# Sliding-window attention: whole weights against the preceding values, a difference of values for the block's own, sinks as a 129th column, queries spread by transfers

## Chip, core and metric

One core of a Trainium2 chip runs the whole two-layer network in one launch. The metric is the device time of the launch in microseconds (us), median of several runs; everything is float32 or its rounded matmul form float32r ("fp32r").

## What is computed

The program is a two-layer decoder over 1024 tokens of width 1024: a gated linear recurrence with a gated convolutional FFN, then sliding-window attention with a second such FFN. The change touches only the attention of layer 2:

```
q = (h @ w_q)                          # 16 heads of 64; keys and values are shared by 4 heads each
for each block of 128 queries:         # keys of this block and of the block before it
    logits = q k^T / 8 + bias[dist]    # only keys at distance 0..127 count
    m      = max(logits.max(), sink)   # one learned sink per head
    p      = exp(logits - m)
    o      = (p @ v) / (p.sum() + exp(sink - m))
out = o @ w_out
```

A query at place t of its block sees keys 0..t of its own block and keys t+1..127 of the block before: exactly 128 keys in all. So one 128x128 tile per block and head holds all the weights, and each column s of it belongs to the own block where s <= t and to the preceding block where s > t.

## The kernel before

**Precision.** A float32 product is three fp32r matmuls (`mm3`) of a rounded high part and a low part of each operand; a low part is made by VectorE (DVE) as source minus high part (L149), the high part by a cast on ScalarE (ACT). Products of weights and values are plain float32 matmuls (`mm32`, L180).

**Attention, by head pairs and block pairs.** `c` (0 to 7) counts pairs of heads, `e` is the head in the pair (partitions 64e to 64e+63), `bp` (0 to 3) counts pairs of 128-query blocks. A step is n = 4c + bp, 32 in all. `attend(c, bp, q)` is a generator of seven stages for a step:

1. TensorE (PE): scores of 2 heads x 2 blocks in a PSUM tile (L1212, 8 matmuls; operands `q` and `QB` are the stationary ones); ACT copies the own block's half to the tile `X` (L1215).
2. DVE lays the preceding block's scores over it where s > t (`copy_predicated`, L1219); GpSimd (POOL) adds the bias (L1225). For bp = 0 there is a block with no predecessor, cut by an `affine_select`.
3. DVE: row maxima (L1230), and a small operation that takes the sink in (L1233); POOL, or DVE for c > 5, forms sink minus maximum (L1234); ACT: four exponentials with row sums in `dn` (L1237), one of the sinks (L1239).
4. DVE adds the sink's part to `dn` (L1241), takes the reciprocal and multiplies `X` (L1243).
5. PE transposes `X` four times into a PSUM tile `pt` (L184).
6. DVE multiplies `pt` by two triangles (L1251, twice): weights of the own block in `W[:, 0]`, of the preceding one in `W[:, 1]`.
7. PE multiplies both by the values `Vt` (16 matmuls, L180); ACT copies the result to `Y` (L1264).

**Order.** PE, ACT, DVE and POOL run in the order written in the code. In step n stand: stage 1 of n, stage 7 of n-3, stage 3 of n-1, stage 2 of n, stages 5 and 6 of n-2, half of a filler, stage 4 of n-1, `q_split` if a query half is done, `make_lows` (deferred low parts), at bp = 0 `q_unit(c+2)`, the other half of the filler. Filler is the projection of the queries of c+1: six matmuls of 512 columns at a time; half h of it ends two steps after it began. After step 20 there is more of the next stage's work: weights of the output projection (`out_unit`, steps 21 to 24) and splits of `Y` (`Y_to_T`, steps 26 to 30). SyncE (SP) issues the DMAs; its order is the scheduler's.

**Queries.** `q_split` takes a projected half from PSUM (head e in partitions 64e..) and makes two stationary operands: `q[:, e]` holds the high part of head e in both partition halves, `QB[:, e]` the low part in one half and zeros in the other. `K` has the high part of the keys in head e's partitions and the low part in the others, so two matmuls give the three products. That is two ACT copies, two DVE operations and two ACT copies more, each on 64 partitions (L1195, L1197, L1200). Half 0 of c+1 is split in step 4c+2 and first used in step 4c+4; half 1 is split in step 4c+4 and used in step 4c+6.

**Weights.** `q_unit` loads the weights of one c by SP into one of three tiles `raw` in turn (`load`, L144), ACT casts them to a slot of `HL` (L156), and DVE makes the low part in the next step's `make_lows`. `HL` has six slots, handed out by `ring["hl"]`.

Of the kernel before, what the change touches and what calls it, by code (L numbers as in the profile page):

```python
# [35 lines left out]
def constant_arrays():  # L36
# [9 lines left out]
    tri = np.zeros((P, 2, P), np.float32)  # L46
    tri[:, 0] = s <= t
    tri[:, 1] = s > t
# [39 lines left out]
def trunk(ctx: ExitStack, tc: tile.TileContext, a: dict, out: bass.AP):  # L88
# [21 lines left out]
    cp.tile([P, 88], F32, name="pad1")  # L110
# [29 lines left out]
    def load(loads):  # L140
        raw = tail["raw"][ring["raw"] % 3]
        ring["raw"] += 1
        for view, src in loads(raw):
            nc.sync.dma_start(view, src)  # L144
        return raw
# [956 lines left out]
    with (tc.tile_pool(name="ta", bufs=1, reuse_waits="tile") as raws,  # L1102
# [7 lines left out]
        tri = at.tile([P, 2, P], F32, name="tri")  # L1110
# [3 lines left out]
        nsk = at.tile([P, 16], F32, name="nsk")  # L1114
        nc.gpsimd.tensor_scalar(nsk, sk, -1.0, None, op0=ALU.mult)
        at.tile([P, 96], F32, name="pad")
        place["hf"] = lambda tb: at.tile([P, KC, P], F32, name="q", bufs=3)
        rows = []
        for v in (a["ln_ffn_g"][0], a["ln_ffn_b"][0]):
            rows.append([at.tile([P, 512], F32, name="X", bufs=4) for _ in range(2)])  # L1120
# [5 lines left out]
        Vt = at.tile([P, NB, 256], F32, name="Vt")  # L1126
        khl, uv = [], []
# [63 lines left out]
        def q_split(q, ps):  # L1191
            heads = [(slice(64 * e, 64 * e + 64), slice(64 - 64 * e, 128 - 64 * e)) for e in range(2)]
            qh, ql = q
            for e, (es, os) in enumerate(heads):
                nc.scalar.activation(qh[es, e, :], ps[es], AF.Copy, scale=0.125)  # L1195
            for e, (es, os) in enumerate(heads):
                nc.vector.scalar_tensor_tensor(ql[es, e, :], ps[es], 0.125, qh[es, e, :].bitcast(F32),  # L1197
                                               op0=ALU.mult, op1=ALU.subtract)
            for e, (es, os) in enumerate(heads):
                nc.scalar.activation(qh[os, e, :], ps[es], AF.Copy, scale=0.125)  # L1200

        def attend(c, bp, q):
# [11 lines left out]
            X = at.tile([P, 2, 2, P], F32, name="X", bufs=4)  # L1214
            nc.scalar.copy(X, pv[:, :, :, P:])  # L1215
            yield
# [11 lines left out]
            se = sm.tile([P, 2, 2], F32, name="se")  # L1228
            dn = sm.tile([P, 2, 2], F32, name="dn")
            nc.vector.tensor_reduce(nm, X, axis=mybir.AxisListType.X, op=ALU.max)  # L1230
            skv = sk[:, 8 * pp + r:8 * pp + r + 5:4].unsqueeze(2).to_broadcast([P, 2, 2])
            nsv = nsk[:, 8 * pp + r:8 * pp + r + 5:4].unsqueeze(2).to_broadcast([P, 2, 2])
            nc.vector.scalar_tensor_tensor(nm, nm, -1.0, nsv, op0=ALU.mult, op1=ALU.min)  # L1233
            (nc.vector if c > 5 else nc.gpsimd).tensor_tensor(se, skv, nm, op=ALU.add)  # L1234
            for e in range(2):
                for jj in range(2):
                    nc.scalar.activation(X[:, e, jj, :], X[:, e, jj, :], AF.Exp, bias=nm[:, e, jj:jj + 1],  # L1237
                                         accum_out=dn[:, e, jj:jj + 1])
            nc.scalar.activation(se, se, AF.Exp)  # L1239
            yield  # L1240
            nc.vector.tensor_tensor(dn, dn, se, op=ALU.add)  # L1241
# [8 lines left out]
            for k in range(2):  # L1250
                nc.vector.tensor_tensor(W[:, k], pt.rearrange("p (g s) -> p g s", g=4),  # L1251
# [46 lines left out]
        def make_lows():  # L1298
            while lows:
                lows.pop(0)()  # L1300
# [119 lines left out]
```

## Time and profile before

| | us |
|---|---|
| median of 3 runs (2201.86 to 2205.51) | 2202.15 |
| the profiled execution, its own time | 2201.14 |
| its span, first to last instruction | 2199.3 |
| attention's steps: first scores at 1284.06, last scores at 1462.80 | 178.7 |

PE is busy for 98% of the span, DVE 81%, ACT 43%, POOL 8%; PE's granted clock is 0.999 of full speed. PE's busy time is a union of overlapping matmuls: a 512-column matmul is shown as 0.39 us long while the next begins 0.23 us later, so a short wait between two can lie under the end of the first. Times below are from the span's start.

### The profile page before, as it was taken

To read this page: it belongs to the slowest core of one execution; us is meant where nothing else is said; L and a number is where in the kernel's file an instruction comes from. 1 tells how busy PE (TensorE), PEld (TensorE's weight loads), DVE (VectorE), ACT (ScalarE), POOL (GpSimd) and SP (SyncE) were. 2 spreads that over 40 slices of the span, in tenths; PEclk is the share of its full clock that TensorE was granted. 3 is DMA by queue.
4 is the path that set the end of the run, shared out by engine and by line. 5 is a ranking of instruction groups with operands and counts; after the bars stand their busy time and mean duration, and the time that the engine had idled before them with its cause. 6 is when DMAs were issued, how large, how long until landed. Compare 5 with 4: busy or idle time off the path is not lost.

```text
span 2199.3 us, 33413 instructions
## 1 busy us (share of the span) xinstructions
PE 2154.9 (98%) x13135; PEld 1813.7 (82%) x13135; DVE 1782.7 (81%) x2415; ACT 942.3 (43%) x1625; POOL 179.3 (8%) x200
## 2 busy tenths in 40 slices
PE   8999999999999999999999999999999999999998
PEld 7888888978888888887888888778788888887887
DVE  2777666565789988888998778887799888889987
ACT  4333322342744433344344356764654443343431
POOL 0122111120100000000000012211000000000001
PEclk9999999999999999999999999999999999999999
DMA  5554443152222222238854421114222222249663
GB/s 198 191 194 173 154 173 116 59 127 93 86 82 86 87 86 86 87 99 271 281 168 134 115 90 35 35 56 140 74 96 94 77 78 87 87 147 318 205 215 134
DMA packets 231945, 281.16 MB, mean 128 GB/s; under 512 B 29978, under 2 KB 160747, under 8 KB 228971
## 3 DMA queue, kind: packets, MB, share of 16 engines
q1 hardware_dynamic: 228736, 276.53, 38.3%
q10 hardware_dynamic: 3050, 2.49, 0.9%
q8 instruction: 103, 1.69, 0.3%
q14 instruction: 56, 0.45, 0.1%
HBM read 213.96 MB, written 65.01 MB: 127 GB/s over the span
## 4 chain that ended last, share of the span: by engine, by line
PE 68%; DVE 18%; ACT 5%; DMA 4%; issue 3%; POOL 1%; SPq 0%; ACTq 0%; DVEq 0%; POOLq 0%
PE psmm L174 14%; PE psmm L176 14%; PE psmm L175 14%; PE psax L174 7%; PE psax L176 7%; PE psax L175 7%; PE psax L180 3%; DVE T L149 3%; DVE HL L149 2%; DVE Y L647 1%; PE psax L184 1%; ACT T L201 1%; DMA rx<-in_ffn_w_in_dram 1%; ACT Y L249 1%; DVE Y L599 1%
## 5 line engine op out<-in xcount | busy, mean ns | idle before, releaser
L174 PE MATMUL psmm<-T,HL 128*128 128x512 f32 x768 | 306.9, 400 | 0.0
L175 PE MATMUL psmm<-T,HL 128*128 128x512 f32 x768 | 299.4, 390 | 4.2 <-DVE T L149 2.8
L176 PE MATMUL psmm<-T,HL 128*128 128x512 f32 x768 | 299.5, 390 | 0.0
L479 DVE SCALAR_TENSOR_TENSOR Y<-Y,cwt 128x1023 f32<-128x1023 f32 (+1 forms) x176 | 225.1, 1279 | 39.5 <-ACT Y L477 39.3
L477 ACT ACTIVATE Y<-Y,cwt 128x1024 f32<-128x1024 f32 x88 | 108.9, 1238 | 257.4 <-DVE Y L466 254.5
L174 PE MATMUL psmm<-HL,T 128*128 128x256 f32 (+1 forms) x656 | 199.7, 304 | 2.4 <-ACT T L201 2.4
L176 PE MATMUL psmm<-HL,T 128*128 128x256 f32 (+1 forms) x656 | 195.2, 298 | 2.4 <-DVE T L149 2.4
L175 PE MATMUL psmm<-HL,T 128*128 128x256 f32 (+1 forms) x656 | 195.0, 297 | 1.2 <-DVE HL L149 1.2
L201 ACT CAST HL<-rx 128x1024 fp32r<-128x1024 f32 (+1 forms) x137 | 140.3, 1047 | 122.0 <-DMA rx<-in_ffn_w_in_dram 33.6
L149 DVE TENSOR_TENSOR HL<-rx,HL 128x1024 fp32r<-128x1024 f32 (+1 forms) x137 | 165.6, 1212 | 15.3 <-ACT HL L201 14.9
L176 PEld LDWEIGHTS psmm<-T,HL 128*128 128x128 f32 x768 | 144.2, 188 | 32.5 <-issue 1.7
L175 PEld LDWEIGHTS psmm<-T,HL 128*128 128x128 f32 x768 | 144.5, 188 | 30.9 <-DVE T L149 3.5
L174 PEld LDWEIGHTS psmm<-T,HL 128*128 128x128 f32 x768 | 144.3, 188 | 30.3 <-issue 1.2
L174 PE MATMUL psax<-T,HL 128*128 128x512 f32 x352 | 137.3, 390 | 0.0
L176 PE MATMUL psax<-T,HL 128*128 128x512 f32 x352 | 137.0, 389 | 0.0
L175 PE MATMUL psax<-T,HL 128*128 128x512 f32 x352 | 136.9, 389 | 0.0
L174 PEld LDWEIGHTS psmm<-HL,T 128*128 128x128 f32 x656 | 126.1, 192 | 9.2 <-ACT T L201 3.0
L176 PEld LDWEIGHTS psmm<-HL,T 128*128 128x128 f32 x656 | 126.0, 192 | 6.6 <-DVE T L149 3.4
L175 PEld LDWEIGHTS psmm<-HL,T 128*128 128x128 f32 x656 | 126.2, 192 | 4.9 <-DVE HL L149 1.7
L223 POOL TENSOR_TENSOR rs<-rs,nhalf 128x1 f32<-128x1 f32 x32 | 25.7, 805 | 1281.1 <-DVE rs L222 1280.8
L858 POOL TENSOR_TENSOR kp<-kp,tot 128x512 f32<-128x512 f32 x48 | 73.8, 1538 | 288.3 <-PE psax L180 147.9
L201 ACT CAST HT<-rx 128x1024 fp32r<-128x1024 f32 (+1 forms) x51 | 44.0, 862 | 89.0 <-PE psmm L175 29.9
(296 smaller groups left out, 5312.7 us busy)
## 6 DMA issues: line engine op xcount, KB each, us to landing
rx<-in_ffn_w_in_dram SPq DMA_DIRECT2D x136, 256.0 KB, 3.2
rx<-gd SPq DMA_DIRECT2D x118, 256.0 KB, 3.6
Y<-in_ffn_w_out_dram SPq DMA_DIRECT2D x44, 512.0 KB, 6.4
bsd<-Y SPq DMA_DIRECT2D x22, 1024.0 KB, 4.4
gd<-Y SPq DMA_DIRECT2D x44, 512.0 KB, 2.6
rx<-in_ffn_w_out_dram SPq DMA_DIRECT2D x54, 256.0 KB, 4.1
R<-bsd SPq DMA_DIRECT2D x44, 256.0 KB, 4.4
Y<-in_ffn_w_in_dram SPq DMA_DIRECT2D x40, 256.0 KB, 3.0
```

Source lines behind the costliest of these rows:

```text
L149: make = lambda e: e.tensor_tensor(lo, src, hi.bitcast(F32), op=ALU.subtract)
L174: nc.tensor.matmul(ps, st(0), mv(0), start=start, stop=False)
L175: nc.tensor.matmul(ps, st(0), mv(1), start=False, stop=False)
L176: nc.tensor.matmul(ps, st(1), mv(0), start=False, stop=stop)
L180: nc.tensor.matmul(ps, lhsT, rhs, start=start, stop=stop, **kw)
L184: nc.tensor.transpose(ps, src, ident)
L201: nc.scalar.copy(hi, src)
L223: nc.gpsimd.tensor_tensor(rs, rs, nhalf, op=ALU.pow)
L249: nc.scalar.activation(hf[:, kc, :], ps[:, k * P:(k + 1) * P], AF.Identity, bias=shift, scale=scale)
L477: nc.scalar.activation(c, u, AF.Identity, bias=cwt[:, l, 3, ci:ci + 1], scale=cwt[:, l, 2, ci:ci + 1])
L479: nc.vector.scalar_tensor_tensor(c[:, sh:], u[:, :S - sh], cwt[:, l, 2 - sh, ci:ci + 1], c[:, sh:], op0=ALU.mult, op1=ALU.add)
L858: (nc.gpsimd if i else nc.vector).tensor_tensor(kv[:, :, 0, :], kv[:, :, 0, :], tv[:, :, 1:2].to_broadcast([P, nb, m]), op=ALU.mult)
```

## The change

Weights: with p the whole tile, the output is p @ V_prev + (own part of p) @ (V_own - V_prev). So `W[:, 1]` becomes a plain copy of `pt` by ACT, `W[:, 0]` stays DVE's product with a triangle, and the own block's values are replaced by a difference `Vd`, which POOL makes once. PE's first matmul of a pair now takes `W[:, 1]`, and the number of matmuls is the same.

Sinks: `X` gets a 129th column, written by POOL, which holds the sink; the maximum runs over 129 columns and is negated by the operation itself, and the exponential's row sum takes the sink in. L1233, L1234, L1239 and L1241 go.

Queries: ACT copies the high part of both heads to a tile `M` at once, DVE makes the low part of both in `L` at once, and six SP transfers of 64 partitions x 512 carry them to their places in `q` and `QB`. `M` and `L` are the halves of one of the three `raw` tiles, so two are left for the weights; `QB` moves to slot 5 of `HL`, so five slots are left and the slots are handed out in another sequence.

```
-        raw = tail["raw"][ring["raw"] % 3]
+        raw = tail["raw"][ring["raw"] % len(tail["raw"])]
...
-        QB = [at.tile([P, 2, 512], F32R, name=f"QB{i}") for i in range(2)]
-        for t in QB:
-            for e in range(2):
-                nc.gpsimd.memset(t[64 - 64 * e:128 - 64 * e, e, :].bitcast(F32), 0.0)
+        QB = [hl_at(5)[:, i, :].rearrange("p (e t) -> p e t", e=2) for i in range(2)]
...
+        Vd = at.tile([P, NB - 1, 256], F32, name="Vd")
...
+            j0 = max(2 * tp, 1)
+            nc.gpsimd.tensor_tensor(Vd[:, j0 - 1:2 * tp + 1, :], Vt[:, j0:2 * tp + 2, :], Vt[:, j0 - 1:2 * tp + 1, :],
+                                    op=ALU.subtract)
...
-            ring["hl"] = (2, 3, 4, 5, 0, 1, 4, 5)[c]
+            ring["hl"] = (2, 3, 4, 0, 1, 2, 3, 4)[c]
...
         def q_split(q, ps):
-            heads = [(slice(64 * e, 64 * e + 64), slice(64 - 64 * e, 128 - 64 * e)) for e in range(2)]
             qh, ql = q
-            for e, (es, os) in enumerate(heads):
-                nc.scalar.activation(qh[es, e, :], ps[es], AF.Copy, scale=0.125)
-            for e, (es, os) in enumerate(heads):
-                nc.vector.scalar_tensor_tensor(ql[es, e, :], ps[es], 0.125, qh[es, e, :].bitcast(F32),
-                                               op0=ALU.mult, op1=ALU.subtract)
-            for e, (es, os) in enumerate(heads):
-                nc.scalar.activation(qh[os, e, :], ps[es], AF.Copy, scale=0.125)
+            M, L = [place["ML"][:, 512 * i:512 * i + 512] for i in range(2)]
+            nc.scalar.activation(M.bitcast(F32R), ps, AF.Copy, scale=0.125)
+            nc.vector.scalar_tensor_tensor(L.bitcast(F32R), ps, 0.125, M, op0=ALU.mult, op1=ALU.subtract)
+            for e in range(2):
+                es, os = slice(64 * e, 64 * e + 64), slice(64 - 64 * e, 128 - 64 * e)
+                for dst, src in ((qh[es, e, :], M), (qh[os, e, :], M), (ql[es, e, :], L)):
+                    nc.sync.dma_start(dst.bitcast(F32), src[es])
...
-            X = at.tile([P, 2, 2, P], F32, name="X", bufs=4)
+            XS = at.tile([P, 2, 2, 144], F32, name="X", bufs=4)
+            X, XS = XS[:, :, :, :P], XS[:, :, :, :P + 1]
             nc.scalar.copy(X, pv[:, :, :, P:])
+            nc.gpsimd.tensor_copy(XS[:, :, :, P], sk[:, 8 * pp + r:8 * pp + r + 5:4].unsqueeze(2).to_broadcast([P, 2, 2]))
...
-            nc.vector.tensor_reduce(nm, X, axis=mybir.AxisListType.X, op=ALU.max)
...
-            nc.vector.scalar_tensor_tensor(nm, nm, -1.0, nsv, op0=ALU.mult, op1=ALU.min)
-            (nc.vector if c > 5 else nc.gpsimd).tensor_tensor(se, skv, nm, op=ALU.add)
+            nc.vector.tensor_reduce(nm, XS, axis=mybir.AxisListType.X, op=ALU.max, negate=True)
...
-                    nc.scalar.activation(X[:, e, jj, :], X[:, e, jj, :], AF.Exp, bias=nm[:, e, jj:jj + 1],
+                    nc.scalar.activation(XS[:, e, jj, :], XS[:, e, jj, :], AF.Exp, bias=nm[:, e, jj:jj + 1],
                                          accum_out=dn[:, e, jj:jj + 1])
-            nc.scalar.activation(se, se, AF.Exp)
             yield
-            nc.vector.tensor_tensor(dn, dn, se, op=ALU.add)
...
-            for k in range(2):
-                nc.vector.tensor_tensor(W[:, k], pt.rearrange("p (g s) -> p g s", g=4),
-                                        tri[:, k, :].unsqueeze(1).to_broadcast([P, 4, P]), op=ALU.mult)
+            nc.vector.tensor_tensor(W[:, 0], pt.rearrange("p (g s) -> p g s", g=4),
+                                    tri.unsqueeze(1).to_broadcast([P, 4, P]), op=ALU.mult)
+            nc.scalar.copy(W[:, 1], pt.rearrange("p (g s) -> p g s", g=4))
...
-                    mm32(o, Vt[:, j, kvc:kvc + 64], W[:, 0, 2 * e + jj, :], stop=j == 0)
+                    mm32(o, Vt[:, max(j - 1, 0), kvc:kvc + 64], W[:, 1, 2 * e + jj, :], stop=j == 0)
                     if j:
-                        mm32(o, Vt[:, j - 1, kvc:kvc + 64], W[:, 1, 2 * e + jj, :], start=False)
+                        mm32(o, Vd[:, j - 1, kvc:kvc + 64], W[:, 0, 2 * e + jj, :], start=False)
...
             hl = q_unit(1)
             make_lows()
+            place["ML"] = tail["raw"][ring["raw"] % 3]
+            tail["raw"] = [t for t in tail["raw"] if t is not place["ML"]]
```

How the instructions stand now is shown at three places. The first is ACT's queue in step 8, a step with a query split. Before:

```order
L1215 COPY X<-psax 128x512
L1264 COPY Y<-psmm 128x256
L1237 ACTIVATE X,dn<-X,nm 128x128 x4
L1239 ACTIVATE se<-se 128x4
L1195 ACTIVATE q<-psmm 64x512 x2
L1200 ACTIVATE q<-psmm 64x512 x2
L156 CAST HL<-raw_10081 128x1024
```

In the changed kernel the same step on ACT, with the engines or DMA semaphores that each instruction waits for in brackets (`raw_10082` is the tile of `M` and `L`):

```order
L1212 COPY X<-psax 128x4x128 [waits PE_49]
L1255 COPY Y<-psmm 128x256 [waits PE_49]
L1230 ACTIVATE X,dn<-X,nm 128x129 [waits DVE_49]
L1230 ACTIVATE X,dn<-X,nm 128x129 x3
L1243 COPY Y<-psmm 128x512 [waits DVE_49,Activation_49]
L1191 ACTIVATE raw_10082<-psmm 128x512 [waits DMAHW6_49,DMAHW4_49,DMAHW7_49,DMAHW3_49,Activation_49]
L154 CAST HL<-raw_10081 128x1024 [waits DMAHW2_49]
```

The exponential of the sinks and four query copies went; a copy of the transposed weights, which waits for DVE's product from the same PSUM tile, and one query copy, which waits for the four transfers that read `M` last, came. The second place is DVE's queue in such a step. Before:

```order
L1230 TENSOR_REDUCE nm<-X 128x4
L1233 SCALAR_TENSOR_TENSOR nm<-nm,nsk 128x4
L1219 COPY_PREDICATED X<-msk,psax 128x128 x2
L1251 TENSOR_TENSOR Y<-psmm,tri 128x512 x2
L1241 TENSOR_TENSOR dn<-dn,se 128x4
L1242 RECIPROCAL dn<-dn 128x4
L1243 TENSOR_TENSOR X<-X,dn 128x512
L1197 SCALAR_TENSOR_TENSOR QB_10086<-psmm,q 64x512 x2
```

and in the changed kernel:

```order
L1227 TENSOR_REDUCE nm<-X 128x4
L1217 COPY_PREDICATED X<-msk,psax 128x128 x2
L1241 TENSOR_TENSOR Y<-psmm,tri 128x512
L1233 RECIPROCAL dn<-dn 128x4
L1234 TENSOR_TENSOR X<-X,dn 128x4x128
L1192 SCALAR_TENSOR_TENSOR raw_10082<-psmm,raw_10082 128x512
```

Two small operations went, the product with a triangle and the query operation stand once in place of twice, and the order is otherwise the same. The third place is SP's queue around one step in four: loads of the bias (`bf`) and of the query weights. Before:

```order
L272 DMA h2d<-Y 128x1024 x3
L144 DMA raw_10082<-in_swa_w_q_dram 128x8x64 x2
L1162 DMA bf<-rbd 128x2x128
L144 DMA raw_10083<-in_swa_w_q_dram 128x8x64 x2
L1162 DMA bf<-rbd 128x2x128
L144 DMA raw_10081<-in_swa_w_q_dram 128x8x64 x2
```

and in the changed kernel (`HL<-raw_10082` is `QB`, now a slot of `HL`):

```order
L1159 DMA bf<-rbd 128x2x128
L1196 DMA q<-raw_10082 64x512 x2
L1196 DMA HL<-raw_10082 64x512
L1196 DMA q<-raw_10082 64x512 x2
L1196 DMA HL<-raw_10082 64x512
L142 DMA raw_10083<-in_swa_w_q_dram 128x8x64 x2
```

The six transfers of a split stand in the program's order between the loads, and the loads use two tiles in turn in place of three.

More of the change, by code (lines that the diff above doesn't have):

```diff
@@ L1119, in trunk @@
         for v in (a["ln_ffn_g"][0], a["ln_ffn_b"][0]):
-            rows.append([at.tile([P, 512], F32, name="X", bufs=4) for _ in range(2)])
+            rows.append([at.tile([P, 576], F32, name="X", bufs=4)[:, :512] for _ in range(2)])
             for h in range(2):
@@ L1315, in trunk @@
             k_part(1)
+            for e in range(2):
+                nc.gpsimd.memset(hl_at(5).rearrange("p i (e t) -> p i e t", e=2)[64 - 64 * e:128 - 64 * e, :, e, :]
+                                 .bitcast(F32), 0.0)
             g = q_proj(hl)
```

15 lines of the change are left out of this document (4 added, 11 removed).

## Prediction

> **What bounds the kernel now.** I read the page first, then the windows of the attention, the waits there, and the starts of the score matmuls in PE's timeline. The windows give, for each stretch: its length, then busy time of PE, its weight loads, DVE, ACT and POOL, PE's granted clock, the DMA share and GB/s.
>
> ```profile
> 1307.00:1331.00 24.00, 23.51 (x177) 19.54 (x176) 20.21 (x45) 16.43 (x57) 7.03 (x11) 1.00 0.12 29
> 1427.00:1451.00 24.00, 21.41 (x151) 17.56 (x151) 22.24 (x46) 17.43 (x54) 6.06 (x6) 1.00 0.00 1
> 1463.00:1475.00 12.00, 11.43 (x88) 8.98 (x87) 10.48 (x23) 7.13 (x24) 1.29 (x1) 1.00 0.00 0
> 1283.00:1475.00 192.00, 183.82 (x1298) 153.43 (x1297) 163.91 (x349) 132.53 (x430) 51.51 (x72) 1.00 0.11 32
> ```
>
> PE is nearly full, at full clock; its visible gaps are 192.00 - 183.82 = 8.2 us. DVE is the engine nearest to it, and in steps 24 to 29 (second row) it works 22.24 of 24 us, with PE down to 21.41. The waits say who holds whom (total us, times, longest):
>
> ```profile
> ACT q L1200 <- DVE QB L1197: 23.2, 15, 1.7
> ACT X L1237 <- DVE nm L1233: 20.3, 15, 2.4
> DVE X L1219 <- ACT X L1215: 16.4, 13, 1.9
> PEld psmm L180 <- DVE W L1251: 7.5, 15, 1.3
> PE psmm L180 <- DVE W L1251: 4.0, 10, 1.1
> ```
>
> PE waits for one thing above all: the weights `W` from DVE. Ahead of it lies a chain: ACT waits inside the query split for DVE, comes late to the copy of X, DVE waits for that copy and makes W late. All PE lost is seen in the starts of the scores:
>
> ```profile
> 1306.49 0.22 PE L1212 MATMUL psax<-K,q 128*128 128x128 f32 x1
> 1311.84 0.28 PE L1212 MATMUL psax<-K,q 128*128 128x256 f32 x1
> 1323.29 0.28 PE L1212 MATMUL psax<-K,q 128*128 128x256 f32 x1
> 1328.45 0.22 PE L1212 MATMUL psax<-K,q 128*128 128x128 f32 x1
> 1357.24 0.28 PE L1212 MATMUL psax<-K,q 128*128 128x256 f32 x1
> 1358.28 1.14 PE L180 MATMUL psmm<-Y,Vt 128*64 128x128 f32 x16
> 1359.36 0.66 PE L184 MATMUL psmm<-ident,X 128*128 128x128 f32 x4
> 1362.61 0.28 PE L1212 MATMUL psax<-K,q 128*128 128x256 f32 x1
> 1396.22 0.22 PE L1212 MATMUL psax<-K,q 128*128 128x128 f32 x1
> 1462.80 0.28 PE L1212 MATMUL psax<-K,q 128*128 128x256 f32 x1
> ```
>
> These are steps 4, 5, 7, 8, 13 (three rows), 14, 20 and 31. Without a wait a step takes 1311.84 - 1306.49 = 5.35 us from bp 0, 1362.61 - 1357.24 = 5.37 from bp 1 and bp 2, and 1328.45 - 1323.29 = 5.16 from bp 3, so four take 21.25. From step 4 to step 31 that makes 6 x 21.25 + 5.35 + 2 x 5.37 = 143.6 us; the trace has 1462.80 - 1306.49 = 156.3. **12.7 us are waits**, 4.7 of them before step 20 (89.7 against 85.0) and 8.0 after. They are more than the visible gaps, since a short wait hides under the modelled end of a matmul. PE's own work does not shrink, so 12.7 us, and some 1.5 us of gaps behind step 31, are all that can be won.
>
> **What goes and what comes, engine by engine.** The rows of the groups (count | busy us, mean ns):
>
> ```profile
> L1197 DVE SCALAR_TENSOR_TENSOR QB<-psmm,q 64x512 fp32r<-64x512 f32 x30 | 20.6, 685 | 1.7 <-ACT q L1195 1.2
> L1251 DVE TENSOR_TENSOR Y<-psmm,tri 128x512 f32<-128x512 f32 x32 | 20.5, 683 | 0.0
> L1241 DVE TENSOR_TENSOR dn<-dn,se 128x4 f32<-128x4 f32 x32 | 9.6, 301 | 3.1 <-ACT se L1239 2.9
> L1233 DVE SCALAR_TENSOR_TENSOR nm<-nm,nsk 128x4 f32<-128x4 f32 x32 | 5.2, 163 | 1.1
> L1200 ACT ACTIVATE q<-psmm 64x512 fp32r<-64x512 f32 x30 | 17.8, 594 | 23.6 <-DVE QB L1197 23.2
> L1195 ACT ACTIVATE q<-psmm 64x512 fp32r<-64x512 f32 x30 | 17.6, 586 | 1.7 <-PE psmm L176 1.6
> L1239 ACT ACTIVATE se<-se 128x4 f32<-128x4 f32 x32 | 6.2, 193 | 0.0
> L1215 ACT COPY X<-psax 128x512 f32<-128x512 f32 x32 | 18.7, 585 | 3.7 <-PE psax L1212 3.4
> L1237 ACT ACTIVATE X<-X,nm 128x128 f32<-128x128 f32 x128 | 49.9, 395 | 20.4 <-DVE nm L1233 20.3
> ```
>
> DVE loses half of L1197 (10.3 us), one product of the two (20.5), L1241 (9.6) and L1233 (5.2): 45.6 of 163.9 us, and in a step with a split 0.69 + 0.68 + 0.30 + 0.16 = 1.8 us. ACT loses L1200, half of L1195 and L1239 (17.8 + 8.8 + 6.2 = 32.8) and gains 32 copies of 128x512, priced by L1215 (18.7): 14.1 us less. What matters more is that ACT no longer waits for DVE inside the split (23.2 us), so the cast and the next copy of X come some 3 us earlier in a step with a split. The 129th column adds 1 part in 128 to L1237 and the maximum, under 0.01 us each. POOL's sink copy stands for L1234; four differences of values and two memsets fall into stretches in which POOL is at 7.03 of 24. If that cover went, each costs about what POOL's bias addition of like size does, and four of those are no more than 5 us once.
>
> Does PE then run without waits? I walk one step, T being the start of its scores. PE by the rows of step 13: values at T+1.04, transposes T+2.12 to 2.78, next scores T+5.37. ACT: copy of X T+1.15 to 1.74, copy of Y behind the values T+2.2, four exponentials at 0.39 each T+2.5 to 4.1, copy of the weights T+4.1 to 4.7, M (starts are 0.5 apart) T+4.6 to 5.2. DVE: product with the triangle T+2.8 to 3.5, reciprocal behind the exponentials, X multiplied by T+5.1, L T+5.2 to 5.9. The next step's PE wants the weights at T+5.37+1.04 = 6.4 (ready 4.7) and the transposes' X at 7.5 (ready 5.1). So 1.7 and 2.4 us of slack take the place of the wait for W. The copy of the weights waits for DVE's product from the same PSUM tile, done at 3.5, before ACT is free at 4.1: nothing.
>
> **The transfers are what is late next.** Behind M on SP stand six issues of 64x512, 128 KB each, and no row shows one from SBUF to SBUF. The nearest are the loads of `swa_w_out`, of the same 64x512 shape; the other rows are ends (issue: ns min/median/max; the DMA rows: KB, us from issue to landing):
>
> ```profile
> L144 SPq DMA_DIRECT2D raw<-in_swa_w_out_dram x16: 465/588/596, 1366.3 to 1419.7; - x16
> L272 SPq DMA_DIRECT2D h2d<-Y x8: 319/320/339, 1240.3 to 1291.0; - x8
> 1366.30 2.46 SPq L144 DMA_DIRECT2D raw<-in_swa_w_out_dram  x4
> raw<-in_swa_w_out_dram SPq DMA_DIRECT2D x16, 128.0 KB, 2.6
> rx<-in_swa_w_out_dram SPq DMA_DIRECT2D x16, 128.0 KB, 3.8
> out_dram<-Y SPq DMA_DIRECT2D x2, 256.0 KB, 2.0
> ```
>
> Four issues in 2.46 us, the last 0.59 long, are 0.62 apart. So the first starts at T+5.2, the sixth at T+8.3, and it lands at T+10.9. It is needed two steps on, by the third score matmul (0.26 in, eight take 1.04): at T+10.98 from bp 0 (5.35 + 5.37) and T+10.79 from bp 2 (5.37 + 5.16). That is just in time, 0.1 late in half of the 14 splits inside the loop: +0.7 us. By the ends of the rows the sixth lands between T+9.5 (issues of 0.32 behind L, landing 2.6) and T+12.1 (0.62 and 3.8); I take the row of the same shape.
>
> The Trainium skill (DMA: Bandwidth & Descriptors, Anatomy of one DMA) gives about 2.0 us fixed plus the bytes over 436 GB/s, for another issuing engine; for 128 KB that is an estimate of 2.3 us. By it no split would be late and the sum would be 0.7 us lower; the row's 2.6 decides.
>
> Two places cost more, once each. **The start:** nothing but the other half's projection covers the first split.
>
> ```profile
> 1278.82 1.20 ACT L1195 ACTIVATE q<-psmm 64x512 fp32r<-64x512 f32 x2 [3.19 <-PE psmm L176]
> 1280.05 1.41 DVE L1197 SCALAR_TENSOR_TENSOR QB<-psmm,q 64x512 fp32r<-64x512 f32 x2 [0.16 <-ACT q L1195]
> ```
>
> L ends at 1280.74, the third issue follows, the sixth starts at 1282.6 and lands at 1285.2, against first scores at 1284.06 + 0.26: +0.9. **Two raw tiles for three, steps 22 to 24:** the third load of output weights waits for its tile until DVE's low part late in step 22, stands on SP behind that step's split (until T+8.9, T of step 22), issues for 2.46 us and lands at about T+13.4. ACT wants to cast it at T+10.1 and stands 3.3 us, the next split's M is some 2 us late, and so are the scores of step 26: +2.0.
>
> **The sum.** -12.7 + 0.7 + 0.9 + 2.0 = -9.1 us. Behind the attention PE's work and the loads, which start at its end, only move with it. From the profiled execution's own time 2201.14 that gives 2192.0. That execution lies 1.0 us under the median of the runs, 2202.15, so for a median I say **2193.0**.
>
> **The rivals.**
> A, slower: the queries land late. With 3.8 us to land, the loads' price when other transfers are in flight, the sixth lands at T+12.1, 1.2 us late on the mean in 14 splits (17), the start costs 2.1 and the two tiles 3.2: -12.7 + 17 + 2.1 + 3.2 = +9.6, 2211.7. It decides from a landing of about 3.15 us on, where each split is 0.55 late. For it: no row shows such a transfer, and the slack is nil. Against: DMA share is 0.12, and all sixteen loads in the attention took about 2.6. Chance 0.20.
> B, cheap transfers: issues of 0.32 apart. All 14 splits land in time, the start costs 0.1 and the two tiles 1.2: -11.4, 2190.7. Chance 0.20.
> C, the gain stays under other waits (the order of ACT and DVE on one PSUM tile, POOL's bias, a PSUM slot): if half of 12.7 remains, -6.4 + 3.6 = -2.8, 2199.3. Against: the slacks above. Chance 0.12.
> D, the six transfers go one after the other, each landing before the next moves: 6 x 2.6 behind T+5.2 is T+20.8, 9.9 late, 14 times: about 2340. Against: the four issues of 2.46 us with 2.6 to land each. The Trainium skill (DMA: Bandwidth & Descriptors, Rules for kernel authors) says that transfers to two partition halves serialize on the shared engines; the four loads go to two halves and show no such time. Chance 0.02.
>
> **How the numbers follow.** The forecast has 0.46. A measurement here can tell about 0.2%, 4.4 us, from no change. Faster: forecast and B, 0.66; same: C, 0.12; slower: A and D, 0.22. The range runs from 2188 (all 12.7 and the 1.5 behind step 31 won) to 2210 (C, and A up to near its price); about half of A and all of D, 0.12, lie above it.
>
> **What would show it.** Right: steps of 5.2 to 5.4 us, DVE under 19 of 24, no wait of L180 for W, the split's sixth transfer landing within 0.3 us of the scores, one long step at 25. Wrong: scores waiting a microsecond or more for DMA in every second step (A); scores never near the landing (B); transposes or values waiting for ACT's copy, or steps still near 5.65 (C).

## The result, and the profile after

The changed kernel takes 2198.11 us (median of 11 runs, 2196.49 to 2202.84) against 2203.38 for the kernel before in the same sessions (11 runs, 2201.86 to 2206.31). The ratio is 0.9976, with a 95% interval of 0.9967 to 0.9985: 5.3 us faster, between 3.3 and 7.3. Forecast were 9.1 us, in the same direction.

The profiled execution of the changed kernel has 2199.59 us and a span of 2197.8, only 1.5 us under that of the kernel before. At its last scores it was 5.3 us ahead (1457.52 against 1462.80). It lost most of its lead in the second feed-forward part, where the kernels do the same work: by the count of matmuls still to come it was 5.8 us ahead at 1980 us and 1.5 at 2010. In the windows of the changed kernel there (length, busy PE, weight loads, DVE, ACT, POOL, granted clock, DMA share, GB/s) one stretch stands out:

```profile
1980.00:1990.00 10.00, 10.00 (x46) 8.29 (x45) 9.96 (x10) 3.16 (x3) 0.00 (x0) 1.00 0.98 361
1990.00:2000.00 10.00, 7.42 (x25) 5.44 (x24) 8.22 (x8) 3.14 (x3) 0.00 (x0) 0.77 0.82 278
```

PE runs 25 matmuls in place of 46 and the clock is granted at 0.77. The 11 runs of this one kernel spread over 6.4 us. So I compare kernels by the ratios of their medians, and look inside the attention by the distance of one score matmul to the next, which such a place later on does not touch.

The attention's windows:

```profile
1307.00:1331.00 24.00, 22.88 (x165) 19.24 (x164) 15.54 (x30) 14.33 (x49) 7.32 (x12) 1.00 0.50 116
...
1427.00:1451.00 24.00, 22.76 (x160) 18.77 (x159) 18.70 (x35) 17.46 (x58) 8.39 (x11) 1.00 0.37 87
...
1283.00:1475.00 192.00, 185.60 (x1330) 156.16 (x1329) 127.00 (x233) 120.82 (x386) 56.05 (x81) 1.00 0.43 107
```

DVE falls from 163.91 to 127.00 us, ACT from 132.53 to 120.82, and PE is busy for 1.8 us more of the same 192. DVE in the late stretch stands at 18.70 of 24, where it was 22.24. The waits of the same part (total us, times, longest):

```profile
PEld psmm L178 <- ACT Y L1243: 2.6, 2, 1.8
PE psax L1208 <- DMA q<-raw: 2.3, 5, 0.9
PE psmm L178 <- ACT Y L1243: 2.2, 2, 1.6
PE psax L1208 <- DMA HL<-raw: 1.4, 5, 0.4
```

No wait of the values (L178, before L180) for DVE is left. In its place stand waits for ACT's copy of the weights and ten for transfers. The score starts in PE's timeline:

```profile
1283.33 0.22 PE L1208 MATMUL psax<-K,q 128*128 128x128 f32 x1
...
1307.67 0.22 PE L1208 MATMUL psax<-K,q 128*128 128x128 f32 x1
1314.57 0.28 PE L1208 MATMUL psax<-K,q 128*128 128x256 f32 x1
...
1351.69 0.22 PE L1208 MATMUL psax<-K,q 128*128 128x128 f32 x1
1358.05 0.28 PE L1208 MATMUL psax<-K,q 128*128 128x256 f32 x1
...
1395.17 0.22 PE L1208 MATMUL psax<-K,q 128*128 128x128 f32 x1
...
1421.73 0.28 PE L1208 MATMUL psax<-K,q 128*128 128x256 f32 x1
1428.78 0.28 PE L1208 MATMUL psax<-K,q 128*128 128x256 f32 x1
1435.50 0.28 PE L1208 MATMUL psax<-K,q 128*128 128x256 f32 x1
...
1457.52 0.28 PE L1208 MATMUL psax<-K,q 128*128 128x256 f32 x1
```

These are steps 0, 4, 5, 12, 13, 20, 25, 26, 27 and 31. From the first to the last it is 174.19 us, before 178.74 (1284.06 to 1462.80): 4.55 gained, and 0.5 more behind step 31. Most steps take 5.16 to 5.37 us, as forecast without waits. Five do not: step 4 takes 6.90, step 12 6.36, step 25 7.05, step 26 6.72, step 28 6.13; and the start, steps 0 to 3, takes 24.34 against 22.43. Three places explain them.

**The start.** Step 0 takes 4.73 us, before 3.67: its scores wait twice for transfers of the very first split, 0.26 us and then 0.42:

```profile
1284.64 0.30 PE L1208 MATMUL psax<-K,HL 128*128 128x128 f32 x1 [0.42 <-DMA HL<-raw]
```

The rest is lost further on. DVE's timeline, then POOL's and SP's queue:

```profile
1298.46 2.30 DVE L147 TENSOR_TENSOR HL<-raw,HL 128x1024 fp32r<-128x1024 f32 x1
```

```profile
1298.38 1.30 POOL L1148 TENSOR_TENSOR Vd<-Vt 128x512 f32<-128x512 f32 x1 [0.39 <-ACT Vt L1146]
1299.63 1.19 POOL L1213 COPY X<-sk 128x4 f32<-128x4 f32 x1
```

```profile
1307.12 0.59 SPq L1196 DMA_DIRECT2D HL<-raw  x1
```

The last difference of values runs beside a low part of DVE's, and that takes 2.30 us where it took 1.22. The exponentials behind it come 1.1 us later, with them ACT's M, and the sixth transfer of the split ahead of step 4 is issued at 1307.12, when step 4 is all but due.

**Late issues.** SP's queue at the split ahead of step 12:

```profile
1346.30 1.11 SPq L1196 DMA_DIRECT2D q<-raw  x2
1347.51 0.54 SPq L1196 DMA_DIRECT2D HL<-raw  x1
1348.09 2.41 SPq L1196 DMA_DIRECT2D q<-raw  x2
1350.60 0.55 SPq L1196 DMA_DIRECT2D HL<-raw  x1
```

The same two issues take 1.24 us in most splits and 2.41 here; in the split ahead of step 28 it is 2.15. The transfer behind is late by as much. This is no accident of one execution: in each of the seven profiled kernels with six transfers a split, these same two splits hold an issue of 1.0 to 2.0 us.

**Two raw tiles.** SP's queue, then ACT in steps 24 and 25, then PE:

```profile
1414.79 5.03 SPq L142 DMA_DIRECT2D raw<-in_swa_w_out_dram  x8
```

```profile
1420.57 1.05 ACT L154 CAST HL<-raw 128x1024 fp32r<-128x1024 f32 x1 [4.94 <-DMA raw<-in_swa_w_out_dram]
...
1423.82 0.57 ACT L1243 COPY Y<-psmm 128x512 f32<-128x512 f32 x1
1424.28 0.60 ACT L1191 ACTIVATE raw<-psmm 128x512 fp32r<-128x512 f32 x1
```

```profile
1424.45 0.45 PE L178 MATMUL psmm<-Y,Vt 128*64 128x128 f32 x4 [1.61 <-ACT Y L1243]
```

ACT stands 4.94 us for the third load of output weights. The copy of the weights is behind that on ACT, and PE waits 1.61 us for it in step 25. M comes late as well, and step 26's queries with it.

### The profile page after: what moved, and what is told of

It is laid out like the page before. It is cut to its first block, busy times and chain, and to the rows that moved or that the text cites. A ratio compares the mean times of both kernels' runs of the same rounds, so it can differ in the third digit from the quotient of the medians.

```text
span 2197.8 us, 33422 instructions
## 1 busy us (share of the span) xinstructions
PE 2156.2 (98%) x13135; PEld 1815.5 (83%) x13135; DVE 1743.4 (79%) x2295; ACT 926.8 (42%) x1577; POOL 187.3 (9%) x209
## 4 chain that ended last, share of the span: by engine, by line
PE 80%; DVE 10%; DMA 3%; ACT 3%; issue 2%; SPq 1%; POOL 1%; ACTq 0%; DVEq 0%; POOLq 0%
PE psmm L172 16%; PE psmm L173 16%; PE psmm L174 16%; PE psax L174 8%; PE psax L172 8%; PE psax L173 8%; PE psax L178 3%; DVE T L147 2%; PE psmm L178 1%; PE psax L1208 1%; PE psax L182 1%; ACT T L199 1%; ACT Y L247 1%; DVE Y L477 1%; DVE HL L147 1%
## 5 line engine op out<-in xcount | busy, mean ns | idle before, releaser
L147 DVE TENSOR_TENSOR HL<-raw,HL 128x1024 fp32r<-128x1024 f32 x51 | 65.3, 1280 | 19.8 <-ACT HL L154 19.8
```

The costliest lines, as they stand in the source:

```text
L147: make = lambda e: e.tensor_tensor(lo, src, hi.bitcast(F32), op=ALU.subtract)
```

## The experiments

Theory 1 was that the steps come free because DVE has less to do, and that the transfers bring losses of their own (start, two raw tiles, late issues). Theory 2, from my prediction, was that what frees them is ACT's wait inside the split (23.2 us before). All runs were compared with the kernel before on the same chip. The slot of `HL` for `QB`, with five slots left for the weights, and the wider rows of `X` (144 columns) stay in all the variants. The table gives the ratio with its interval, what it makes of 2204 us, and the time from the first scores to the last in the profiled execution, less the 178.74 of the kernel before ("by the scores" below).

| kernel | ratio (95%) | us | first to last scores |
|---|---|---|---|
| the whole change | 0.9976 (0.9967, 0.9985) | -5.3 | -4.55 |
| transfers alone, 64 bytes off | 1.0010 (1.0001, 1.0019) | +2.2 | -6.92 |
| transfers alone, aligned | 0.9968 (0.9956, 0.9980) | -7.1 | -7.32 |
| column alone | 0.9957 (0.9944, 0.9971) | -9.5 | -9.52 |
| whole weights alone | 1.0032 (1.0019, 1.0044) | +7.1 | +6.28 |
| column and whole weights | 0.9983 (0.9974, 0.9993) | -3.7 | -2.56 |
| the same, ACT first | 0.9979 (0.9970, 0.9988) | -4.6 | -2.90 |
| transfers and column | 0.9954 (0.9942, 0.9967) | -10.1 | -9.55 |
| the same, three raw tiles | 0.9940 (0.9928, 0.9951) | -13.2 | -11.77 |
| the same, low part in place | 0.9946 (0.9933, 0.9958) | -11.9 | -12.88 |
| column, ACT first | 0.9967 (0.9954, 0.9979) | -7.3 | -6.70 |
| whole change, last difference on DVE | 0.9974 (0.9960, 0.9988) | -5.7 | -5.59 |
| whole change, one more issue | 1.0001 (0.9992, 1.0009) | +0.2 | +2.27 |

With one exception the two last columns agree to 2.1 us, about what the intervals leave open.

### The split undone

```diff
-            M, L = [place["ML"][:, 512 * i:512 * i + 512] for i in range(2)]
...
-                    nc.sync.dma_start(dst.bitcast(F32), src[es])
+            for e, (es, os) in enumerate(heads):
+                nc.scalar.activation(qh[es, e, :], ps[es], AF.Copy, scale=0.125)
+            for e, (es, os) in enumerate(heads):
+                nc.vector.scalar_tensor_tensor(ql[es, e, :], ps[es], 0.125, ...)
+            for e, (es, os) in enumerate(heads):
+                nc.scalar.activation(qh[os, e, :], ps[es], AF.Copy, scale=0.125)
...
-            tail["raw"] = [t for t in tail["raw"] if t is not place["ML"]]
```

> The change with its query split undone: two ACT copies, two DVE products, two ACT copies as before, no transfers, three raw tiles; whole weights, difference of values and the 129th column stay. Theory 1 (the transfers brought in their own losses, some 9 us: start 3.5, two raw tiles 3, late issues 1.8; DVE's smaller load by itself frees the steps): attention steps of 5.2 to 5.4 us, time 8 to 11 us under the kernel before. Theory 2 (what freed the steps is that ACT no longer waits for DVE inside the split): ACT still waits over 15 us there, steps stay near 5.65 us with PE waiting for W, time within 4 us of the kernel before.

Measured: 3.7 us under the kernel before, as theory 2 had it. Its waits:

```profile
ACT q L1197 <- DVE HL L1194: 23.6, 16, 1.5
...
PEld psmm L178 <- ACT W L1244: 12.0, 14, 1.7
```

ACT still waits 23.6 us in the split, and PE waits for the weights. But it waits for ACT's copy of them (L1244), not for DVE. So there were two suspects: the wait in the split, and the whole weights' copy on ACT.

### ACT first

```diff
             for e, (es, os) in enumerate(heads):
                 nc.scalar.activation(qh[es, e, :], ps[es], AF.Copy, scale=0.125)
+            for e, (es, os) in enumerate(heads):
+                nc.scalar.activation(qh[os, e, :], ps[es], AF.Copy, scale=0.125)
             for e, (es, os) in enumerate(heads):
                 nc.vector.scalar_tensor_tensor(ql[es, e, :], ps[es], 0.125, ...)
-            for e, (es, os) in enumerate(heads):
-                nc.scalar.activation(qh[os, e, :], ps[es], AF.Copy, scale=0.125)
```

> As the split undone, but all four ACT copies of the split stand ahead of DVE's two products, so ACT waits for nobody there. Theory 1: 10 to 12 us under the kernel before, no wait of ACT for DVE inside the split. Theory 2: the same, and 6 us or more better than the split undone in the old order. Rival: ACT, with some 1.8 us more work in a step with a split, becomes late for the copy of X, and the steps with a split grow by 0.5 us or more (time less than 5 us under the kernel before).

Measured: 4.6 us under. ACT's wait inside the split is gone, but DVE now waits there for ACT's copies:

```profile
DVE HL L1196 <- ACT q L1194: 28.6, 16, 1.9
```

The time hardly moves: steps 8, 12, 16 and 20 take 5.54 to 5.56, PE waits 5.7 us for the copy of the weights, and a step at the end takes 9.0. Both theories were wrong on this run, theory 2 in its main point. The rival's time came (less than 5 us), its longer steps with a split did not.

### Transfers alone

The whole weights, the difference of values and the column are undone; the split by transfers stays. Against the changed kernel:

```diff
-            nc.vector.tensor_reduce(nm, XS, axis=mybir.AxisListType.X, op=ALU.max, negate=True)
+            nc.vector.tensor_reduce(nm, X, axis=mybir.AxisListType.X, op=ALU.max)
+            nc.vector.scalar_tensor_tensor(nm, nm, -1.0, nsv, op0=ALU.mult, op1=ALU.min)
...
-            nc.scalar.copy(W[:, 1], pt.rearrange("p (g s) -> p g s", g=4))
+            for k in range(2):
+                nc.vector.tensor_tensor(W[:, k], pt..., tri[:, k, :]..., op=ALU.mult)
```

> Only the query spread by transfers (two raw tiles, query lows in HL's last slot); two triangle products and the sink's own maximum, sum and exponential as before. Theory 1 (transfers cost some 8 us and DVE's load must fall too): half of the 12.7 us of waits stays, so -6 + 8 = about +2, from -1 to +5 us against the kernel before. Theory 2 (the split's wait is what cost PE time): all steps between the start and the last loads at 5.2 to 5.4 us, time 3 to 6 us under the kernel before, like the whole change.

Measured: 2.2 us over the kernel before, inside theory 1's range, but not for its reason. Most steps are at 5.15 to 5.35 and the scores need 6.9 us less; 9 us were lost where no edit was. The small tiles of the sink's sum are back in this kernel, and 64 bytes more lay ahead of what follows. So one more run, with the padding of the kernel before:

```diff
-    cp.tile([P, 104], F32, name="pad1")
+    cp.tile([P, 88], F32, name="pad1")
```

> Transfers alone again, with the padding ahead of the tiles at 88 floats as in the kernel before, not 104: the small tiles of the sink's sum take 64 bytes, and with both the later tiles lie 64 bytes further on. Theory 1 (that shift slows matmuls outside the attention by some 0.8% and hid the gain): matmuls of the first feed-forward part again 0.227 us apart throughout, time 5 to 8 us under the kernel before, as the attention's steps say. Rival (the 9 us lie elsewhere, in the load or the profile): time within 2 us of the first run of transfers alone, 0 to 4 us over the kernel before.

Measured: 7.1 us under, as theory 1 said. The windows of the first feed-forward part, first of the kernel that is 64 bytes off, then of the aligned one (PE's count of matmuls is in the first bracket):

```profile
700.00:1000.00 300.00, 300.00 (x1315) 246.38 (x1314) 266.35 (x297) 123.05 (x141) 0.00 (x0) 1.00 0.28 89
```

```profile
700.00:1000.00 300.00, 300.00 (x1326) 248.39 (x1325) 267.67 (x299) 124.45 (x143) 0.00 (x0) 1.00 0.29 91
```

1315 against 1326 matmuls in 300 us, with PE busy throughout and the clock full in both. In the second part it is 1314 against 1325 in another 300 us.

### Column alone, whole weights alone

Of the whole change only the sinks' column is left in the first kernel, only the weights and the difference of values in the second; the split is as before, with three raw tiles. Against the kernel before, the first and the second:

```diff
-            nc.vector.scalar_tensor_tensor(nm, nm, -1.0, nsv, op0=ALU.mult, op1=ALU.min)
-            (nc.vector if c > 5 else nc.gpsimd).tensor_tensor(se, skv, nm, op=ALU.add)
+            nc.vector.tensor_reduce(nm, XS, axis=mybir.AxisListType.X, op=ALU.max, negate=True)
...
```

```diff
-            for k in range(2):
-                nc.vector.tensor_tensor(W[:, k], pt..., tri[:, k, :]..., op=ALU.mult)
+            nc.vector.tensor_tensor(W[:, 0], pt..., tri..., op=ALU.mult)
+            nc.scalar.copy(W[:, 1], pt.rearrange("p (g s) -> p g s", g=4))
...
```

> Only the sinks as 129th column; split by ACT and DVE in the old order, two triangle products, three raw tiles. Theory 1 (the whole weights and the difference of values cost more than they save: their copy stands on ACT, which is late, and the values wait for it): 4 to 6 us under the kernel before, at least as good as column and whole weights together, which came 3 to 4 us under it. Rival (whole weights relieve DVE and carry the gain of that run): 0 to 2 us under the kernel before.

> Only the whole weights with the difference of values; split and sinks as before, three raw tiles, padding as in the kernel before. Theory 1 (they cost: the copy of weights comes on top of ACT's wait in the split, and DVE loses only 0.7 us a step): from 1 us under to 4 us over the kernel before. Rival (DVE's product was what PE waited for): 4 us or more under the kernel before.

Measured: the column alone 9.5 us under the kernel before, the whole weights alone 7.1 over it; both beyond theory 1, and far from the rivals. The waits of the column alone:

```profile
ACT q L1195 <- DVE HL L1192: 22.2, 15, 1.5
...
ACT X L1229 <- DVE nm L1226: 10.6, 10, 2.0
...
PE psmm L180 <- DVE W L1241: 1.1, 5, 0.4
```

The starts of steps 4 and 20:

```profile
1306.34 0.22 PE L1207 MATMUL psax<-K,q 128*128 128x128 f32 x1
...
1391.24 0.22 PE L1207 MATMUL psax<-K,q 128*128 128x128 f32 x1
```

They are 84.90 us apart, where 85.0 is a stretch without waits and 89.73 it was before. ACT still waits 22.2 us inside the split, and steps 4 to 23 take 5.16 to 5.37 all the same. So the wait need not go for these steps to come free: by itself it cost PE nothing there, and theory 2 is wrong as it stood. It is one way all the same, for transfers alone take the wait away, leave the sinks' work, and have steps 5 to 23 but for step 12 at 5.16 to 5.37 too. What the column leaves, 3.4 us, lies in steps 24, 26, 28 and 29 (6.08 to 6.38), and no run tells whether that wait or DVE's work there holds them. And of the weights alone:

```profile
ACT q L1199 <- DVE HL L1196: 23.6, 16, 1.5
...
PEld psmm L178 <- ACT W L1252: 17.9, 13, 2.4
...
PE psmm L178 <- ACT W L1252: 15.2, 13, 2.2
```

Here PE waits for ACT's copy 15.2 us (before, 4.0 for DVE's product). This kernel also answers a question on the column's: it has `QB` in `HL` and the wide rows of `X` too, and column and whole weights together differ from it by the column alone. That difference is 10.8 us (-3.7 against +7.1; 8.8 by the scores), so the gain is the column's own.

### The change without whole weights

```diff
-            nc.vector.tensor_tensor(W[:, 0], pt..., tri..., op=ALU.mult)
-            nc.scalar.copy(W[:, 1], pt.rearrange("p (g s) -> p g s", g=4))
+            for k in range(2):
+                nc.vector.tensor_tensor(W[:, k], pt..., tri[:, k, :]..., op=ALU.mult)
```

with the values met as before, and no difference of values.

> The change without its whole weights and difference of values: DVE makes both triangle products, values as before; transfers and 129th column stay. Theory 1 (the difference of values on POOL slows DVE's low part at 1298 us from 1.22 to 2.30 us and so the second split by 1.1 us; DVE has slack for one more product of 0.68 us a step): the start costs 2 us less, steps stay at 5.2 to 5.4 us, time 6 to 8 us under the kernel before. Rival (DVE's load decides): steps with a split grow by 0.3 us or more, time within 3 us of the kernel before.

Measured: 10.1 us under the kernel before, more than theory 1 said. Steps stay at 5.16 to 5.37 with both products on DVE, against the rival, and four of the five long steps shrink: step 4 to 5.93, 12 to 5.57, 25 to 5.37, 28 to 5.42; step 26 keeps 6.45. Next to it, with a tile of its own for M and L, so that three raw tiles stay:

```diff
-            place["ML"] = tail["raw"][ring["raw"] % 3]
-            tail["raw"] = [t for t in tail["raw"] if t is not place["ML"]]
+        place["MLt"] = at.tile([P, 1024], F32, name="ML")
...
+            place["ML"] = place["MLt"]
```

> Transfers and 129th column without whole weights and difference of values, and with a tile of its own for the halves of the query, so that three raw tiles stay. Theory 1 (in the run without the difference, step 26 takes 6.45 us instead of 5.37, and only because the third load of output weights waits for a raw tile): step 26 falls to 5.4 us and the time is 1 us under that run, 10 to 12 us under the kernel before. Rival: step 26 comes from something else, and the time is that run's, 9 to 10 us under.

Measured: 13.2 us under, more than theory 1 said, and step 26 at 5.36. By the scores the third tile is worth 2.2 us: 1.1 in step 26, as said, and 1.2 in the start and step 4, which theory 1 had not named.

### The two terms by themselves

The last difference of values on DVE instead of POOL:

```diff
-            nc.gpsimd.tensor_tensor(Vd[...
+            (nc.vector if tp == 3 else nc.gpsimd).tensor_tensor(Vd[...
```

> The whole change, with the last of the four differences of values (behind the last two value blocks, in step 2) made by DVE instead of POOL. Theory 1 (POOL's difference at 1298.38 us runs beside DVE's low part and is why that takes 2.30 us instead of 1.22; the second split is late by it): the low part takes 1.2 to 1.4 us, step 4 falls from 6.9 to about 5.9 us, time 1 to 2 us under the whole change. Rival (the low part is slow for another reason, or DVE's own 1.3 us for the difference comes to the same): step 4 stays at 6.9 us, time within 0.5 us of the whole change.

Measured: 0.4 us from the whole change, no difference, and step 4 at 7.26: the rival, by its second reason. DVE's timeline and SP's queue:

```profile
1300.84 1.21 DVE L147 TENSOR_TENSOR HL<-raw,HL 128x1024 fp32r<-128x1024 f32 x1
1301.98 0.68 DVE L1148 TENSOR_TENSOR Vd<-Vt 128x512 f32<-128x512 f32 x1
```

```profile
1307.73 1.23 SPq L1196 DMA_DIRECT2D q<-raw  x2
1309.01 0.95 SPq L1196 DMA_DIRECT2D HL<-raw  x1
```

The low part is back at 1.21 us, so POOL's difference beside it was the cause of the 2.30. Of the 1.1 us DVE spends 0.68 on the difference itself, and an issue of 0.95 in place of some 0.55 took the rest. The cause is shown; this cure is none. The Trainium skill (SBUF — State Buffer, Who interferes with whom) says that a DVE instruction with two inputs in SBUF contends with a GpSimd instruction that reads SBUF, and calls the port pair that they share an exclusive lock. The trace agrees: the low part reads raw and HL, the difference reads the values and began 0.08 us earlier, and 2.30 us is 1.21 and 1.09 of POOL's 1.30.

One more transfer ahead of the six:

```diff
+            nc.sync.dma_start(place["pad"][:64, :], M[:64, :112])
```

> The whole change with one more transfer (64x112, into padding) issued ahead of each split's six. Theory 1 (the six land just in time, their last at about 10.5 us behind the scores of the split's step against 10.8 to 11.0 needed): each of 14 splits becomes 0.2 to 0.4 us late, together with the late places (start, step 25) 4 to 7 us over the whole change. Rival (there is slack): less than 1.5 us over the whole change.

Measured: 0.2 us over the kernel before, 5.5 over the whole change (6.8 by the scores). The issue itself took 0.47 us. Steps 4 to 23 need 3.2 us more for ten splits, 0.3 each. So the six do land just in time.

### Versions without late transfers

The column alone, with the edit of "ACT first": ACT's four copies ahead of DVE's two products.

> The 129th column and a split without transfers, with all four ACT copies ahead of DVE's two products; no whole weights, no difference of values; three raw tiles. Theory 1 (ACT's wait inside the split is what the transfers removed, and ACT, without the copies of weights, has room for the four copies): steps of 5.2 to 5.5 us, 10 to 13 us under the kernel before, near the run with transfers and three raw tiles (13 to 14 under). Rival (only leaving the split's second half to the transfers frees ACT and DVE enough): 3 to 6 us under the kernel before, steps with a split 0.3 us or more longer.

Measured: 7.3 us under, between theory 1 and the rival. Steps 4 to 23 are at 5.16 to 5.37, but steps 26, 28 and 29 take 6.45, 6.69 and 8.89. In step 28 DVE's two products wait 1.39 us for ACT's copies, a low part of `T` stands behind them, and PE waits for that:

```profile
1448.69 0.50 PE L176 MATMUL psmm<-HL,T 128*128 128x512 f32 x1 [1.67 <-DVE T L149]
```

Last, transfers and column with three raw tiles and the low half written in place, so that M alone is spread by four transfers:

```diff
-            nc.vector.scalar_tensor_tensor(L.bitcast(F32R), ps, 0.125, M, ...)
+                nc.vector.scalar_tensor_tensor(ql[es, e, :], ps[es], 0.125, M[es], ...)
-                for dst, src in ((qh[es, e, :], M), (qh[os, e, :], M), (ql[es, e, :], L)):
+                for dst, src in ((qh[es, e, :], M), (qh[os, e, :], M)):
```

> Transfers, 129th column, three raw tiles, no difference of values, and the low half written in place by two DVE products of 64x512 instead of one of 128x512 and two transfers: four transfers a split, the last issued 1.2 us earlier. Theory 1 (with three raw tiles only the start and a late issue here and there are left of the transfers' cost): the first step loses the 0.7 us it still has, 0 to 1.5 us under the run with six transfers, 13 to 15 us under the kernel before. Rival (DVE's 0.7 us more in a step with a split brings its waits back): 1 us or more over that run.

Measured: 11.9 us under the kernel before. Steps 4 to 30 all take 5.16 to 5.37, the start is that of the kernel before, and from first to last scores it is 165.86 us, 1.1 less than with six transfers. By the scores that is theory 1, by the times it is the rival's 1 us over that run. Between these two kernels, 13.2 and 11.9 us under, the intervals do not decide; both beat the kernel before and the changed one. Their windows, six transfers first:

```profile
1283.00:1475.00 192.00, 191.23 (x1362) 161.81 (x1361) 143.93 (x265) 105.73 (x354) 52.46 (x80) 1.00 0.46 119
```

```profile
1283.00:1475.00 192.00, 191.72 (x1367) 162.51 (x1366) 157.37 (x284) 106.23 (x354) 54.84 (x80) 1.00 0.36 98
```

PE is busy 191 to 192 of 192 us. DVE does 157.37 us in the second, only 6.5 less than before the change, and ACT 106.23, 26.3 less; with that no step waits.

## Why the prediction came out as it did

**What can be won: right.** I put 12.7 us of waits into steps 4 to 31. The kernel whose steps 4 to 30 are all free of waits needs 12.88 less from first to last scores.

**DVE and ACT: the loads came near, the reason was one of two.** In the window DVE does 36.9 us less (45.6 forecast) and ACT 11.7 less (14.1), though the changed kernel is 5 us further on at the window's end. In the 45.6 I took the row of L1251 into Y for one product of the two; it holds both products of every second step, and half of both rows is 19.9, so the sum hardly moves. Left out was L1234 on DVE, 8 times 0.16 us. I also wrote that what matters more than DVE's load is that ACT no longer waits inside the split. The transfers alone, which take that wait away, do free steps 5 to 23 but for step 12; but the column alone leaves it at 22.2 us, frees the same steps and wins 9.5. Either is enough, and I had named one as the one that matters. The column takes 0.30 + 0.16 us from DVE and 0.19 from ACT in each step, in the run of work from the maximum to the weights; the steps with a split, 6 to 22, had lost 0.47 to 0.86. Removing them is shown to do it, up to step 23. That it is their place in that run, and not DVE's total, I only argue: the whole weights take 0.68 a step from DVE too, and lose; alone, they leave DVE at 143.65 us of the window and the scores take 6.3 us longer.

**The copy of the weights: wrong.** The step that failed is "DVE's product from the same PSUM tile, done at 3.5, before ACT is free at 4.1: nothing". It is nothing while ACT is on time. Against the kernel without whole weights the scores take 5.0 us more (174.19 and 169.19), and this is where: the start with step 4 1.6, step 12 0.8, step 25 1.7, step 26 0.3, step 28 0.7. The copy puts M 0.46 us later in every split, where nothing was to spare; it lets PE wait whenever ACT waits for a load; and the difference of values came beside DVE's low part. For these differences I had named cover on POOL and not asked whom POOL holds up. This one term is what parts forecast and result: without whole weights and differences the change wins 10.1 us, with them 5.3, and 9.1 were forecast. That the rest of the sum fits so well is partly luck: without them start, issues and tiles cost 1.9, 0.3 and 1.1 us by the scores, where I had 0.9, 0.7 and 2.0.

**The terms.** In the sum stood -12.7 + 0.7 + 0.9 + 2.0 = -9.1. The profile has: start and step 4 3.5 (forecast 0.9), splits with late issues 1.8 (0.7), two raw tiles 3.0 (2.0), and 0.5 gained behind step 31. The 0.7 stood for a lateness of 0.1 in every second split. That did not come, steps behind a split take 5.33 and 5.37; the 1.8 is two late issues, which I had not priced. I also had the sixth transfer wanted by the third score matmul; it is the fourth that reads it, 0.12 us later, so the 0.7 was next to nothing by my own figures. The 0.9 itself was right: step 0 takes 1.06 us longer. What I missed is the split ahead of step 4. At the two tiles the mechanism was as walked, with SP free of the split at T+8.9; but ACT's cast began at T+14.7 where I had the load at T+13.4. The load's last issue began at T+10.8, as walked, so it took 3.9 us to the cast and not 2.6; four issues of the next load followed it at once, and whether they held it is not shown. Both the values of step 25 and the queries of step 26 were late.

**The transfers: right within a few tenths.** Step 20 starts its scores at 1395.17. ACT's and SP's timeline show M and the sixth issue of its split, the DMA view the landing:

```profile
1399.65 0.60 ACT L1191 ACTIVATE raw<-psmm 128x512 fp32r<-128x512 f32 x1
```

```profile
1403.40 0.55 SPq L1196 DMA_DIRECT2D HL<-raw  x1
```


```profile
q<-raw SPq DMA_DIRECT2D x64, 128.0 KB, 2.3
HL<-raw SPq DMA_DIRECT2D x32, 128.0 KB, 2.3
```

M is at T+4.5 (4.6 forecast), the sixth issue at T+8.2 (8.3), and it takes 2.3 us to land, not 2.6. Here the estimate of 2.3 from the Trainium skill (DMA: Bandwidth & Descriptors, Anatomy of one DMA) agrees with the trace better than my row of loads did. The transfer lands at T+10.5, 0.2 us ahead of the scores of step 22 at T+10.7. The slack is too small to hold a late issue. Without whole weights M stands 0.46 us earlier, at T+4.02 (step 20 begins at 1396.93 there), and a late issue of 1.47 us (here 1.77) costs step 12 only 0.24 us, not 1.03:

```profile
1400.95 0.58 ACT L1189 ACTIVATE raw<-psmm 128x512 fp32r<-128x512 f32 x1
```

**The rivals.** A did not come: nothing landed at 3.15 us as a rule, though the experiment with one more issue shows how near it was. B is out as a mechanism: the pitch is 0.6, not 0.32. That most splits land in time all the same comes from the landing of 2.3 us. C came in part, under another wait than those I listed; its sign, values waiting for ACT's copy, is there twice, 2.2 us in all. D is out: six transfers, each landing in 2.3 us at a pitch of 0.6. Of the signs of being right, DVE at 18.70 of 24 and a landing close ahead of the scores came; instead of one long step there are five.

## What to carry to other kernels

Split a change into its parts and measure them one by one, the pleasing ones as well: here a column of sinks was worth 9.5 us, the transfers 7 alone and next to nothing on top of it until the third raw tile came back, and the whole weights cost 5 to 7 wherever they stood. A long wait between two engines that are not the bound may cost nothing; look at what stands in the serial run that ends at PE. And work moved to an engine that runs in the order written inherits every wait in front of it there, here 4.94 us on ACT: ask what happens on the day when that engine is late.

## What the runs showed of the hardware

- Of the issues of these transfers, most take 0.46 to 0.6 us; in each of the seven profiled kernels with six transfers a split, two to four take 0.95 to 2.0. In all seven, one of 1.0 to 2.0 us lies in the split ahead of step 12 and one of 1.3 to 1.8 in that ahead of step 28. What holds them is open; no run was made on it.
- A shift of later tiles by 64 bytes slowed matmuls of 128x512 by 0.8%, in a part whose code and order were the same, and cost 9.3 us in all (ratios 1.0010 and 0.9968). By which access is open.
- A POOL difference of 128x512 beside a DVE low part of 128x1024 took that from 1.21 to 2.30 us, and POOL's next copy of 128x4 from 0.65 or 0.19 to 1.19.
